# Attention on one core: head-norm roots spread by a TensorE product, value maxima on VectorE, some high parts on GpSimd

## The chip, the cores and the metric

The kernel runs on one core of a Trainium2 chip. The metric is the device time of one execution in microseconds (us); where several runs exist, their median is taken. The core's engines are TensorE (PE, with its weight loads as PEld), VectorE (DVE), ScalarE (ACT), GpSimd (POOL) and SyncE (SP), which here issues nearly all DMA transfers. Each engine works through its own instructions in the order in which they stand in its queue, and waits on semaphores for the others.

## The reference

The input is 1024 positions of 1024 features. Layer 0 is a recurrent block (RG-LRU) and a squared-ReLU MLP; layer 1 is attention in a band of chunks, with keys and values computed from the stream, and a second MLP. The diff touches the attention alone:

```python
def rmsnorm(x, g):
    y = xf * lax.rsqrt(jnp.mean(xf * xf, axis=-1, keepdims=True) + EPS)
    return (y * g).astype(x.dtype)
...
h = rmsnorm(x, kv_norm)
kv = (h @ w_kv).reshape(bsz, s, 2, N_HEADS, HEAD_DIM)      # 16 heads of 64
k = rmsnorm(kv[:, :, 0], k_norm)                           # norm over each head's 64 features
v = kv[:, :, 1]
...
q = rmsnorm((rmsnorm(h, b_norm[j]) @ b_w_q[j]).reshape(bsz, s, N_HEADS, HEAD_DIM), b_q_norm[j])
# 64-row chunks; each sees 9 chunks of keys (8 to the left and its own)
sc = jnp.einsum('bhqd,bhkd->bhqk', qb, kb) * scale + bias
p = jax.nn.softmax(sc, axis=-1)
o = jnp.einsum('bhqk,bhkd->bhqd', p, vb)
h = h + o @ b_w_o[j]
```

Everything is float32, and the result is the whole stream after the second MLP.

## The kernel before, in words

All activations are held transposed: features on the 128 partitions, positions along the row, in halves of 512 (`H2`). Large products are done in three passes of rounded parts, high x high, low x high and high x low (`mm`, L376 to L378); ACT makes a high part by a rounding copy, and VectorE or GpSimd subtracts it to get the low part.

The attention stage works on eight pairs of heads `t`. For each, `Proj` makes keys, queries and values in this order. Each of the six projections (three kinds, two halves of the positions) is 8 fill steps of three matmuls. `normed` takes a projection of keys or queries out of PSUM (L1726), squares it (L1729, L1732; GpSimd subtracts the low part `sl`, L1735) and adds the sums of squares of each head over the partitions with two matmuls against a band of ones (L1744, L1745). The sums of all four projections of a pair land in one PSUM bank (`nm`; there is one such bank, handed round by the semaphore `nms`), head by head in groups of 16 rows. `roots` makes the reciprocal roots of the bank: ACT Ln, Exp and Square, then two VectorE steps (L1794 to L1805). What remains is to spread each head's row of roots over its 64 partitions. For that L1807 writes eight rows to DRAM (`rd`), and four DMA reads (L1811) bring them back, each row repeated 64 times, as four tiles `rb` of 128 x 512. At L1752 VectorE multiplies the projection with its gain and with `rb`. High and low float16 parts follow (L1762, L1768), and eight small transfers that place the two heads of the pair (`moves`).

`values` takes the value projection out of PSUM (L1686) and lets ACT sum its absolute values over the row (L1689); the two sums, added, bound the largest value and give the scale for the float16 parts (`planes`), which DMA transposes turn (L1668).

A `Unit` is one head (`e`), one half of the queries (`h`) and two blocks of 128 queries (`u`); there are 64. `score` computes the scores of one block `qi` in PSUM (L1963, L1964), adds the bias and takes the row's extreme on VectorE (L1967), takes the exponential on ACT (L1974), and, when both blocks' sums have been inverted (`roots` of the unit, L1990 on VectorE and L1992 on GpSimd), makes the high part `hi` on ACT (L1982) and the low part on VectorE (L1984). Two DMA transposes turn the parts (L1668: `t<-t` for the wide units with `h` = 1, `v<-v` for the others), TensorE weighs the values with them (L2010), and `leave` combines the result (L2021, L2023).

The order in which all engines get their instructions is planned at build time. `Plan` holds a clock for every engine, adds an assumed cost for each step (`c_act`, `c_dve`, `c_pool`, `C_MOVE` for a transfer) and an assumed latency, and issues the steps of all chains in the order of these planned times. `TensorE`'s filler is the row of projection steps (and at its end the first steps of the output projection); a unit is begun when the number of filler steps done reaches its due step and one of `ROWS` tickets is free, which it gives back when its scores are done:

```python
total = 8 * 6 * NF + 2 * JP * (NF - 1)
due = [START]
for c in cost:
    due.append(due[-1] + (total - START - LATE) * c / sum(cost))
```

The plan does not see what a transfer or a wait really takes: an instruction that stands early in its engine's queue holds those behind it.

Tiles come from rings: `g` (64 tiles of 128 x 512, among them `q`, `hr`, `rb`), `w` (14 of the same size, for the weights' parts and short-lived results), `raw` (8), and two rings of 128 x 640 for the scores.

Of the kernel before, what the change touches and what calls it, by code (L numbers as in the profile page):

```python
# [9 lines left out]
F32 = mybir.dt.float32  # L10
# [5 lines left out]
P = 128  # L16
T = 1024
D = 1024
NF = 8
# [15 lines left out]
WIDE = {"nm": 1, "s2": 2}  # L35
PIN = 0
WARM = 9
START = 52
LATE = 12
SLACK = 14  # L40
LOAD_O = 24
SPILL = 5
SPARE = 0.1
ROWS = 3
FR = 0.9
LAT = 0.3
LAT0 = 0.1
# [18 lines left out]

def c_act(n):
    return 0.2 + n * 0.00082


def c_acts(n):
    return 0.28 + n * 0.000836


def c_dve(n):
    return 0.145 + n * 0.00105
# [105 lines left out]
def tile_yoco_rglru_chunk_attention(  # L182
# [43 lines left out]
    def gf(s="g"):  # L226
        return gp.tile([P, H2], F32, tag="g", name=nm(s))
# [22 lines left out]
    def rawf():  # L250
        return rp.tile([P, H2], F32, tag="raw", name=nm("raw"))

    def wr(s="w"):
        return wp.tile([P, H2], F32R, tag="w", name=nm(s))

    def wf():
        return wp.tile([P, H2], F32, tag="w", name=nm("wf"))
# [7 lines left out]
    def bank(tag=None):  # L265
        if tag is None:
            tag = ("pj", "tp", "sc", "pj", "tp", "sc", "po", "sc")[ring[0] % 8]
            ring[0] += 1
        if tag in BANKS:
            return ps1.tile([P, H2], F32, tag=tag, name=nm(tag), bufs=BANKS[tag])  # L270
        return loose.tile([P, H2], F32, tag=tag, name=nm(tag), bufs=(LOOSE if tag in LOOSE else WIDE)[tag])
# [1323 lines left out]
    x1d = dp.tile([NF, P, T], F32, name="x1d")  # L1595
    x2d = dp.tile([NF, P, T], F32, name="x2d")
    x3d = dp.tile([NF, P, T], F32, name="x3d")
    rd = dp.tile([NF, 8, H2], F32, name="rd")
    od = dp.tile([SPILL, 2, P, T], F32, name="od")
    hid = dp.tile([7, NQ, P, H2], F32, name="hid")  # L1600

# [60 lines left out]
    def move(dst, src):  # L1662
        dma(dst, src)
        return plan.use("sp", C_ISSUE) + C_MOVE
# [6 lines left out]
    class Proj:  # L1671


        def __init__(self, t):
            self.t = t
            self.Q = self.K = self.KL = None
            self.rb = [None] * 4
            self.split = [0, 0]
            self.added, self.spread = [Flag(plan) for _ in range(4)], [Flag(plan) for _ in range(4)]
            self.VS, self.V = [None, None], [None, None]  # L1680
            self.made = {(kind, h): Flag(plan) for kind in range(3) for h in range(2)}

        def values(self, h, ps):
            yield scaled[h]
            q = gf("q")
            dve.scalar_tensor_tensor(q, ps, -1.0, R[h], ALU.mult, ALU.mult)  # L1686
            yield plan.use("dve", c_dve(H2))
            m = tiny()
            act.activation(rawf(), q, AF.Abs, accum_out=m)  # L1689
            yield plan.use("act", c_act(H2) + 0.19)  # L1690
            self.V[h] = q, m
            if not h:
                return
            t = self.t
            (_, m0), (_, m1) = self.V
            peak, up = tiny(), tiny()
            dve.tensor_scalar(peak, m0, m1, 1e-20, ALU.add, ALU.max)
            dve.reciprocal(up, peak)
            dve.tensor_scalar(up, up, UP, 1.0, ALU.mult, ALU.mult)
            dve.tensor_scalar(vsc[:, t : t + 1], peak, UP ** -2, 1.0, ALU.mult, ALU.mult)  # L1700
            yield plan.use("dve", 0.45)
            for a, b in SIDES:
                act.activation(vsx[a, t : t + 1], vsc[b, t : t + 1], AF.Copy)
                plan.use("act", 0.2)
            for g in range(2):
                plan.start(self.planes(g, self.V[g][0], up))
# [15 lines left out]
        def normed(self, kind, h, ps):  # L1722
            keys = kind == KEYS
            yield scaled[h]
            q = gf("q")
            dve.scalar_tensor_tensor(q, ps, -1.0, R[h], ALU.mult, ALU.mult)  # L1726
            yield plan.use("dve", c_dve(H2))
            sh = wr("sh")
            act.activation(sh, q, AF.Square)  # L1729
            plan.use("act", c_act(H2))  # L1730
            s = wf()
            act.activation(s, q, AF.Square)  # L1732
            yield plan.use("act", c_act(H2))
            sl = wr("sl")
            SLE.tensor_tensor(sl, s, sh.bitcast(F32), ALU.subtract)  # L1735
            yield plan.use("pool", c_pool(2 * H2), True) if SLE is pool else plan.use("dve", c_dve(H2), True)
            j = 2 * kind + h
            if not j:
                yield nms
                self.ss = bank("nm")  # L1740
            else:
                yield self.added[j - 1]
            ones2 = band[:, 96 - 32 * j : 96 - 32 * j + P]
            pe.matmul(self.ss, lhsT=ones2, rhs=sh, start=j == 0, stop=False, skip_group_check=True)  # L1744
            pe.matmul(self.ss, lhsT=ones2, rhs=sl, start=False, stop=j == 3, skip_group_check=True)  # L1745
            yield plan.pe(2 * H2)
            self.added[j].set(plan.t)
            if j == 3:
                plan.start(self.roots())
            yield self.spread[j]  # L1750
            r = self.rb[j]
            dve.scalar_tensor_tensor(q, q, gk if keys else gq, r, ALU.mult, ALU.mult)  # L1752
            yield plan.use("dve", c_dve(H2), True)
            if keys:
                if not h:
                    self.K, self.KL = (gh("ev"), gh("od")), (gh("lo"), gh("los"))
                even, odd, low, lows = (x[:, hs(h)] for x in (*self.K, *self.KL))
            else:
                if not h:
                    self.Q, self.QL = (gh("ev"), gh("od")), gh("lo")  # L1760
                even, odd, low = (x[:, hs(h)] for x in (*self.Q, self.QL))
            act.activation(even, q, AF.Copy)  # L1762
            ready = plan.use("act", c_act(H2))
            if not keys:
                act.activation(odd[OD], q[OD], AF.Copy)
                plan.use("act", c_act(H2))
            yield ready
            dve.tensor_tensor(low, q, even, ALU.subtract)  # L1768
            yield plan.use("dve", c_dve(H2), True)
            self.split[kind] += 1  # L1770
            if self.split[kind] == 2:
                plan.start(self.moves(kind))
# [19 lines left out]
        def roots(self):  # L1792
            ss, r = self.ss, gf("hr")
            act.activation(r, ss, AF.Ln, scale=1.0 / HD, bias=eps)  # L1794
            yield plan.use("act", c_act(H2))
            act.activation(r, r, AF.Exp, scale=-0.5)
            yield plan.use("act", c_act(H2))
            x = wf()
            act.activation(x, r, AF.Square, scale=(0.5 / HD) ** 0.5)
            yield plan.use("act", c_act(H2))  # L1800
            dve.scalar_tensor_tensor(x, ss, HD * EPS, x, ALU.add, ALU.mult)
            last = plan.use("dve", c_dve(H2))
            nms.release(last)
            yield last
            dve.scalar_tensor_tensor(r, x, 1.5, r, ALU.subtract, ALU.mult)  # L1805
            yield plan.use("dve", c_dve(H2), True)
            move(rd[self.t], r[0:P:16])  # L1807
            yield plan.busy["sp"] + C_MOVE
            for j in range(4):
                self.rb[j] = rb = gf("rb")  # L1810
                last = move(  # L1811
                    rb,
                    rd[self.t, 2 * j : 2 * j + 2].unsqueeze(1).broadcast_to([2, HD, H2]),
                )
                self.spread[j].set(last)
            yield last

# [42 lines left out]
    def weight():  # L1860
# [5 lines left out]
            plan.start(prepare())  # L1866
        return w

    def head_gains():
        yield plan.t  # L1870
        dve.tensor_reduce(
            peaks, hn[:, 2:].rearrange("p (g d) -> p g d", g=2), mybir.AxisListType.X, ALU.max,
            apply_absolute_value=True,
        )
        dve.tensor_scalar(peaks, peaks, 1e-15, 1.0, ALU.max, ALU.mult)
        dve.reciprocal(under, peaks)
        dve.tensor_scalar(gq, hn[:, 0:1], under[:, 0:1], UPN, ALU.mult, ALU.mult)
        dve.tensor_scalar(gk, hn[:, 1:2], under[:, 1:2], -UPN, ALU.mult, ALU.mult)
        dve.tensor_scalar(c1, peaks[:, 0:1], peaks[:, 1:2], UPN ** -2 / 8, ALU.mult, ALU.mult)
        dve.reciprocal(nb, c1)  # L1880
        dve.tensor_scalar(nb, nb, -1.0, 1.0, ALU.mult, ALU.mult)
        yield plan.use("dve", 1.4)
# [10 lines left out]
    class Unit:  # L1893
# [54 lines left out]
        def score(self, qi):  # L1948
# [30 lines left out]
                self.pieces = self.plane(), self.plane()  # L1979
            off = qi * self.count[0] * P  # L1980
            hi, lo = (x[:, off : off + wdt] for x in self.pieces)
            act.activation(hi, sc[:, :wdt], AF.Copy, scale=sm)  # L1982
            yield plan.use("act", c_acts(wdt))
            dve.scalar_tensor_tensor(lo, sc[:, :wdt], sm, hi, ALU.mult, ALU.subtract)  # L1984
            self.scored[qi].set(plan.use("dve", c_dve(wdt) + 0.06, True))

# [395 lines left out]
```

## Time and profile before

| | |
|---|---|
| two runs | 2226.83 and 2232.08 us, median 2229.45 |
| the profiled execution | 2225.27 us, span 2223.2 |
| TensorE busy, matmul | 2027.9 us, 91% of the span |
| VectorE busy | 1490.2 us, 67% |
| ScalarE busy | 1104.1 us, 50% |
| GpSimd busy | 436.3 us, 20% |
| mean granted clock of TensorE | 0.958 |

A row of a list of groups reads: line, engine, operation, output<-input by the program's names, shapes, count, busy time in us, mean ns of one, idle time of the engine before them and what ended it. A row of the order of time reads: start in us, duration, engine, line, operation, and in brackets how long the engine sat idle before it and what released it. A row of the chain that ended last reads: start, duration, what. A row of a table of stretches gives, for each engine, busy us and the number of instructions, then granted clock, DMA share and GB/s. `x11` is a count. For one line's instructions, three durations in ns are least, median and greatest.

### The profile page before, as it was taken

How to read it: one execution, taken by the hardware profiler on the slowest of the kernel's cores; microseconds unless marked ns; L12 is line 12 of the kernel's file. 1: busy time of each engine (PE TensorE's matmuls, PEld its weight loads, DVE VectorE, ACT ScalarE, POOL GpSimd, SP SyncE). 2: the span in 40 equal slices, each digit the busy share in tenths (PEclk: the TensorE clock that was granted, in tenths of full speed). 3: DMA queues.
4: the chain of work that ended last, by engine and by line, in shares of the span. 5: the costliest groups of instructions: out<-in, count | busy, mean ns of one | idle time of the engine just before them, and what ended most of it. 6: DMA issues, size and time to landing. Idle time of an engine off the chain costs nothing.

```text
span 2223.2 us, 27860 instructions
## 1 busy us (share of the span) xinstructions
PE 2027.9 (91%) x9209; PEld 1638.1 (74%) x9209; DVE 1490.2 (67%) x2340; ACT 1104.1 (50%) x1920; POOL 436.3 (20%) x429
## 2 busy tenths in 40 slices
PE   7999999999999999977687769539999999999999
PEld 6888888888888888855465546427888888888887
DVE  6898777666777766345655456357886667777743
ACT  6778454434345455435575457356553434444532
POOL 2000113222200001332443334311123223000000
PEclk9999999999999999988898889869999999999999
DMA  4012435444697835247777656868444444887833
GB/s 156 29 44 83 147 117 182 156 148 146 220 333 241 262 127 176 86 75 121 128 154 142 133 117 154 192 126 188 158 159 152 157 156 157 317 279 243 252 106 104
DMA packets 319297, 357.07 MB, mean 161 GB/s; under 512 B 163952, under 2 KB 166896, under 8 KB 319152
## 3 DMA queue, kind: packets, MB, share of 16 engines
q1 hardware_dynamic: 319008, 355.24, 56.0%
q8 instruction: 72, 1.18, 0.2%
q14 instruction: 73, 0.60, 0.1%
q10 hardware_dynamic: 144, 0.05, 0.0%
HBM read 230.28 MB, written 80.87 MB: 140 GB/s over the span
## 4 chain that ended last, share of the span: by engine, by line
PE 79%; DMA 11%; DVE 3%; SPq 2%; issue 2%; ACT 2%; POOL 2%; DVEq 0%; POOLq 0%; ACTq 0%
PE pj L376 11%; PE pj L377 11%; PE pj L378 11%; PE tp L377 5%; PE tp L378 5%; PE tp L376 5%; DMA rb<-rd 5%; PE p L377 4%; PE sc L376 4%; PE sc L377 4%; PE p L378 4%; PE sc L378 4%; PE p L376 4%; PE po L2010 2%; DMA t<-t 1%
## 5 line engine op out<-in xcount | busy, mean ns | idle before, releaser
L376 PE MATMUL pj<-h,wh 128*128 128x512 f32 x1260 | 511.8, 406 | 7.3 <-ACT h L2032 7.2
L377 PE MATMUL pj<-l,wh 128*128 128x512 f32 x1260 | 497.6, 395 | 0.8 <-DVE l L2034 0.8
L378 PE MATMUL pj<-h,wl 128*128 128x512 f32 x1260 | 497.4, 395 | 0.0
L1140 ACT ACTIVATE wh<-raw 128x512 fp32r<-128x512 f32 x333 | 205.6, 624 | 168.7 <-PE pj L377 43.5
L376 PEld LDWEIGHTS pj<-h,wh 128*128 128x128 f32 x1260 | 242.0, 192 | 59.5 <-ACT h L2032 8.0
L1141 DVE TENSOR_TENSOR wl<-raw,wh 128x512 fp32r<-128x512 f32 x333 | 254.0, 770 | 39.3 <-ACT wh L1140 36.2
L378 PEld LDWEIGHTS pj<-h,wl 128*128 128x128 f32 x1260 | 240.7, 191 | 52.0
L377 PEld LDWEIGHTS pj<-l,wh 128*128 128x128 f32 x1260 | 241.7, 192 | 49.4 <-DVE l L2034 1.5
L389 ACT ACTIVATE h<-raw 128x512 fp32r<-128x512 f32 x224 | 139.3, 628 | 217.5 <-PE sc L377 61.8
L378 PE MATMUL tp<-h,wl 128*128 128x512 f32 x554 | 215.7, 389 | 1.5 <-DVE wl L342 1.5
L377 PE MATMUL tp<-l,wh 128*128 128x512 f32 x554 | 215.8, 389 | 0.3 <-DVE l L390 0.3
L376 PE MATMUL tp<-h,wh 128*128 128x512 f32 x554 | 215.6, 389 | 0.0
L390 DVE TENSOR_TENSOR l<-raw,h 128x512 fp32r<-128x512 f32 x224 | 153.5, 692 | 76.1 <-ACT h L389 73.1
L1415 ACT ACTIVATE s<-s 128x512 f32<-128x512 f32 x125 | 79.0, 633 | 203.7 <-DVE s L1414 195.0
L2010 PEld LDWEIGHTS <-vs 128*128 128x128 f16 x576 | 53.5, 103 | 157.4 <-issue 131.0
L377 PE MATMUL p<-l,wh 128*128 128x512 f32 x384 | 150.7, 392 | 9.3 <-DVE l L672 9.3
L376 PE MATMUL sc<-h,wh 128*128 128x512 f32 x394 | 153.3, 389 | 0.0
L378 PE MATMUL sc<-h,wl 128*128 128x512 f32 x394 | 153.3, 389 | 0.0
L377 PE MATMUL sc<-l,wh 128*128 128x512 f32 x394 | 153.3, 389 | 0.0
L376 PE MATMUL p<-h,wh 128*128 128x512 f32 x384 | 151.1, 393 | 1.0 <-ACT wh L555 1.0
L378 PE MATMUL p<-h,wl 128*128 128x512 f32 x384 | 150.3, 391 | 0.0
L1149 POOL TENSOR_TENSOR raw<-raw,raw 128x512 f32<-128x512 f32 x29 | 49.9, 1721 | 372.1 <-DVE wl L1141 274.0
(323 smaller groups left out, 3599.2 us busy)
## 6 DMA issues: line engine op xcount, KB each, us to landing
raw<-hid SPq DMA_DIRECT2D x224, 256.0 KB
hid<-s SPq DMA_DIRECT2D x221, 256.0 KB
raw<-in_w_down SPq DMA_DIRECT2D x192, 256.0 KB
raw<-in_w_up SPq DMA_DIRECT2D x128, 256.0 KB
s<-in_w_down SPq DMA_DIRECT2D x64, 256.0 KB
raw<-in_w_kv SPq DMA_DIRECT2D x32, 256.0 KB
rb<-rd SPq DMA_DIRECT2D x32, 256.0 KB
raw<-in_w_in SPq DMA_DIRECT2D x30, 256.0 KB
```

Source lines behind the costliest of these rows:

```text
L376: pe.matmul(ps, lhsT=wh, rhs=xh, start=start, stop=False, skip_group_check=more)
L377: pe.matmul(ps, lhsT=wh, rhs=xl, start=False, stop=False, skip_group_check=more)
L378: pe.matmul(ps, lhsT=wl, rhs=xh, start=False, stop=stop, skip_group_check=more)
L389: act.activation(h, src, AF.Copy)
L390: dve.tensor_tensor(l, src, h.bitcast(F32), ALU.subtract)
L1140: act.activation(wh, raw, AF.Copy)
L1141: dve.tensor_tensor(wl, raw, wh.bitcast(F32), ALU.subtract)
L1149: pool.tensor_tensor(raw[A11], raw[A11], raw[A21], ALU.add)
L1415: act.activation(out, out, AF.Square)
L2010: pe.matmul(dst, lhsT=st, rhs=src, start=start, stop=final, skip_group_check=self.u == 1)
```

## The change

The roots no longer go through DRAM. After the last VectorE step of `roots`, ACT rounds the whole tile to a high part `rh`, and one VectorE step forms `rr`: the high part in a group's first eight rows and the remainder, with `lows` = -1, in row 8 of each group of 16. For each of the four projections TensorE then multiplies `rr` with a constant matrix `pick[:, j]`, which has ones where a head's high row and its remainder row meet the head's 64 partitions; the product lands in the `nm` bank, and L1752's VectorE step reads it from there and gives the bank back. `pick` (a tile of the `w` ring, held for the whole stage) and `lows` are built at the start of the stage in `head_gains`.

The largest absolute value comes from a VectorE reduction instead of an ACT sum, and the larger of the two halves' results is taken instead of their sum. The high part of the second block (`qi` = 1) of the units with `h` = 1, 32 steps of 128 x 640, moves from ACT to GpSimd. The first unit is due after 48 filler steps instead of 52, and four units instead of three may be in their score phase.

```diff
-START = 52
+START = 48
-ROWS = 3
+ROWS = 4
+def c_phi(n):
+    return 0.08 + n * 0.001
...
             m = tiny()
-            act.activation(rawf(), q, AF.Abs, accum_out=m)
-            yield plan.use("act", c_act(H2) + 0.19)
+            dve.tensor_reduce(m, q, mybir.AxisListType.X, ALU.max, apply_absolute_value=True)
+            yield plan.use("dve", c_dve(H2))
...
-            dve.tensor_scalar(peak, m0, m1, 1e-20, ALU.add, ALU.max)
+            dve.tensor_scalar(peak, m0, m1, 1e-20, ALU.max, ALU.max)
...
             yield self.spread[j]
-            r = self.rb[j]
+            yield nms
+            r = bank("nm")
+            pe.matmul(r, lhsT=pick[:, j, :], rhs=self.rr, start=True, stop=True)
+            yield plan.pe(H2)
             dve.scalar_tensor_tensor(q, q, gk if keys else gq, r, ALU.mult, ALU.mult)
-            yield plan.use("dve", c_dve(H2), True)
+            last = plan.use("dve", c_dve(H2))
+            nms.release(last)
+            yield last
...
             dve.scalar_tensor_tensor(r, x, 1.5, r, ALU.subtract, ALU.mult)
             yield plan.use("dve", c_dve(H2), True)
-            move(rd[self.t], r[0:P:16])
-            yield plan.busy["sp"] + C_MOVE
+            hi, self.rr = wr("rh"), wr("rr")
+            act.activation(hi, r, AF.Copy)
+            yield plan.use("act", c_act(H2))
+            dve.scalar_tensor_tensor(self.rr, hi.bitcast(F32), lows, r, ALU.mult, ALU.add)
+            last = plan.use("dve", c_dve(H2), True)
             for j in range(4):
-                self.rb[j] = rb = gf("rb")
-                last = move(
-                    rb,
-                    rd[self.t, 2 * j : 2 * j + 2].unsqueeze(1).broadcast_to([2, HD, H2]),
-                )
                 self.spread[j].set(last)
...
+    pick, lows = wr("pick").rearrange("p (j m) -> p j m", j=4), kp.tile([P, 1], F32, name="lows")
     def head_gains():
         yield plan.t
+        where = wf().rearrange("p (j m) -> p j m", j=4)
+        pool.memset(where, 0.0)
+        for low in range(2):
+            for e, half in enumerate((EV, OD)):
+                pool.affine_select(
+                    out=where[:, :, half], in_=where[:, :, half], pattern=[[-32, 4], [0, HD]],
+                    compare_op=ALU.not_equal, fill=1.0, base=-16 * e - 8 * low, channel_multiplier=1,
+                )
+        act.activation(pick, where, AF.Copy)
+        mark = gf("mark")
+        pool.memset(mark[:, :HD], 0.0)
+        pool.affine_select(... fill=-1.0, base=-8, channel_multiplier=1)
+        plan.use("pool", 5.0)
+        dve.tensor_reduce(lows, mark[:, :HD], mybir.AxisListType.X, ALU.add)
...
-            act.activation(hi, sc[:, :wdt], AF.Copy, scale=sm)
-            yield plan.use("act", c_acts(wdt))
+            if h and qi:
+                pool.tensor_scalar(hi, sc[:, :wdt], sm, 1.0, ALU.mult, ALU.mult)
+                yield plan.use("pool", c_phi(wdt), True)
+            else:
+                act.activation(hi, sc[:, :wdt], AF.Copy, scale=sm)
+                yield plan.use("act", c_acts(wdt))
```

More of the change, by code (lines that the diff above doesn't have):

```diff
@@ L1597, in tile_yoco_rglru_chunk_attention @@
     x3d = dp.tile([NF, P, T], F32, name="x3d")
-    rd = dp.tile([NF, 8, H2], F32, name="rd")
     od = dp.tile([SPILL, 2, P, T], F32, name="od")
@@ L1676, in __init__ @@
             self.Q = self.K = self.KL = None
-            self.rb = [None] * 4
             self.split = [0, 0]
@@ L1867, in weight @@
         return w
+    pick, lows = wr("pick").rearrange("p (j m) -> p j m", j=4), kp.tile([P, 1], F32, name="lows")
     def head_gains():
         yield plan.t
+        where = wf().rearrange("p (j m) -> p j m", j=4)
[9 more added lines that the diff above has]
+        pool.memset(mark[:, :HD], 0.0)
+        pool.affine_select(
+            out=mark[:, :HD], in_=mark[:, :HD], pattern=[[-16, 8], [-1, 8]],
+            compare_op=ALU.not_equal, fill=-1.0, base=-8, channel_multiplier=1,
+        )
+        plan.use("pool", 5.0)
+        dve.tensor_reduce(lows, mark[:, :HD], mybir.AxisListType.X, ALU.add)
         dve.tensor_reduce(
```

## The prediction

> **What bounds the kernel now.** I read the page first: the busy tenths, the DMA line under them and the shares of the chain that ended last.
>
> ```profile
> span 2223.2 us, 27860 instructions
> PE   7999999999999999977687769539999999999999
> DMA  4012435444697835247777656868444444887833
> PE pj L376 11%; PE pj L377 11%; PE pj L378 11%; PE tp L377 5%; PE tp L378 5%; PE tp L376 5%; DMA rb<-rd 5%; PE p L377 4%; PE sc L376 4%; PE sc L377 4%; PE p L378 4%; PE sc L378 4%; PE p L376 4%; PE po L2010 2%; DMA t<-t 1%
> ```
>
> TensorE is full everywhere but in slices 18 to 28, about 945 to 1556 us: the attention stage, the only one the diff touches. There the DMA engines are busier than in the slices around it. The chain is TensorE nearly throughout; its largest other item is the transfer `rb<-rd`, the spreading of the head-norm roots that this change removes. Next, the waits of TensorE between 900 and 1600 us and one wait of VectorE (columns: sum in us, times, longest).
>
> ```profile
> PE po L2010 <- DMA t<-t: 76.4, 14, 20.5
> PE po L2010 <- DMA v<-v: 40.3, 9, 18.7
> PE nm L1745 <- POOL sl L1735: 28.6, 6, 16.3
> PE s L1963 <- DVE t L1967: 6.6, 6, 2.4
> DVE q L1752 <- DMA rb<-rd: 119.5, 32, 4.8
> ```
>
> TensorE is said to wait for transposes, not for the roots. The order of time says what lies behind it. These are the waits of TensorE that are longer than 10 us, one for each of the eight head pairs:
>
> ```profile
> 978.69 0.80 PE L1745 MATMUL nm<-sl,band 128*128 128x512 f32 x1 [16.32 <-POOL sl L1735]
> 1040.95 0.80 PE L2010 MATMUL po<-v,vs 128*128 128x256 f16 x4 [12.00 <-DVE o L2023]
> 1108.97 0.37 PE L2010 MATMUL po<-t,vs 128*128 128x256 f16 x1 [16.04 <-DMA t<-t]
> 1179.18 0.37 PE L2010 MATMUL po<-t,vs 128*128 128x256 f16 x1 [14.26 <-DMA t<-t]
> 1260.32 0.37 PE L2010 MATMUL po<-v,vs 128*128 128x256 f16 x1 [15.23 <-DMA v<-v]
> 1324.29 0.40 PE L2010 MATMUL po<-t,vs 128*128 128x256 f16 x1 [16.64 <-DMA t<-t]
> 1408.43 0.37 PE L2010 MATMUL po<-v,vs 128*128 128x256 f16 x1 [18.72 <-DMA v<-v]
> 1483.54 0.37 PE L2010 MATMUL po<-t,vs 128*128 128x256 f16 x1 [20.49 <-DMA t<-t]
> ```
>
> They add up to 129.7 us. I looked into the third, from 1093 to 1109: SyncE's queue, VectorE, and the busy times of that stretch (PE, PEld, DVE, ACT, POOL, then granted clock, DMA share, GB/s).
>
> ```profile
> 1084.02 9.23 SPq L286 DMA_DIRECT2D rb<-rd  x4
> 1093.36 14.69 SPq L1668 DMA_TRANSPOSE t<-t  x2
> 1091.76 0.75 DVE L1752 SCALAR_TENSOR_TENSOR q<-q,gk,rb 128x512 f32<-128x512 f32 x1 [1.34 <-DMA rb<-rd]
> 1107.80 0.75 DVE L1752 SCALAR_TENSOR_TENSOR q<-q,gq,rb 128x512 f32<-128x512 f32 x1 [3.80 <-DMA rb<-rd]
> 1093.00:1109.00 16.00, 0.03 (x1) 0.03 (x1) 4.34 (x8) 1.38 (x3) 1.26 (x1) 0.60 0.88 76
> ```
>
> Four products `q*rb` stand between 1091.76 and 1107.80, so 5.35 us apart: that is the pace at which the four reads of 256 KB land, one behind the other. VectorE works in order and is held by each; SyncE is held for 9.23 us by the four issues and for 14.69 us by the two transposes behind them; TensorE wants those transposes. All five engines stand still, and for one reason.
>
> **What goes.** One `rd` write and four `rb` reads for each pair, 40 transfers, leave SyncE's queue, and four buffers of the g ring are no longer taken. A transpose that has no `rb` reads ahead of it is quick:
>
> ```profile
> 1016.92 3.51 DMA t<-t
> L1668 SPq DMA_TRANSPOSE t<-t x64: 1259/1484/10807, 1005.3 to 1541.6; - x64
> ```
>
> It lands 3.51 us after its start, and half the issues take at most 1.484 us. In the third stall, issued where the reads now are (1084.02), two transposes would land near 1084.0 + 2 x 1.5 + 3.5 = 1090.5, before TensorE arrived at 1092.9. So nothing else was close behind, and I count all eight stalls as gone: **-129.7**. What is late next are the lags of ACT, POOL and DVE, priced below. As the stall holds every engine, none of them used it to catch up with TensorE much, which is why I don't give the time back to them.
>
> After each such stall TensorE is slow for a while. The first two rows are eleven products after a stall and after none, the other two the start of the first and fourth projection product after a stall; behind them, the pace of a full stage.
>
> ```profile
> 1110.10 2.08 PE L2010 MATMUL po<-t,vs 128*128 128x256 f16 x11 [0.75 <-DMA t<-t]
> 1020.47 1.15 PE po L2010 x11
> 1111.93 0.78 PE L376 MATMUL pj<-h,wh 128*128 128x512 f32 x1
> 1113.36 0.42 PE L376 MATMUL pj<-h,wh 128*128 128x512 f32 x1
> 100.00:200.00 100.00, 100.00 (x443) 82.81 (x442) 95.41 (x99) 72.97 (x81) 3.98 (x4) 1.00 0.16 51
> ```
>
> The products cost 2.08 - 1.15 = 0.93 more; three projections take 1.43 instead of 3 x 100/443 = 0.68, 0.75 more. Together 1.68, eight times: **-13.4**.
>
> **What comes on TensorE.** 32 products of 512 columns, of a kind and size with the projections: 32 x 100/443 = **+7.2**, and nothing hides them, TensorE being the chain. Each also adds a wait. The product for j = 0 needs the roots, now with two more steps (the ACT copy `rh` and the VectorE step `rr`); those for j = 1 to 3 need the one `nm` bank back, so the VectorE product before them. Behind such a product on TensorE stand projections, scores and weighings; behind the VectorE step that waits for it stand the subtractions `lo` and all reductions. How late the roots come shows in the last sum of a pair and the end of its roots, in the first pair and in the last:
>
> ```profile
> 943.34 0.40 PE L1745 MATMUL nm<-sl,band 128*128 128x512 f32 x1
> 947.97 0.69 DVE L1805 SCALAR_TENSOR_TENSOR hr<-wf,hr 128x512 f32<-128x512 f32 x1
> 1433.47 0.40 PE L1745 MATMUL nm<-sl,band 128*128 128x512 f32 x1
> 1453.10 0.67 DVE L1805 SCALAR_TENSOR_TENSOR hr<-wf,hr 128x512 f32<-128x512 f32 x1
> ```
>
> With idle engines the roots take 5.3 us (943.34 to 948.66), in the last pair 20.3 (1433.47 to 1453.77). The planner sets the product where it thinks the roots done; only the lag behind its plan is waited out. Where TensorE today depends directly on another engine, the rows of waits give that lag: the five shorter waits for `sl` are (28.6 - 16.3)/5 = 2.5 us, the longest wait of a score for VectorE 2.4. Bounds: nothing, and 20.3 - 5.3 = 15 us for a pair. I take 2.5 for j = 0, the nearest row, and 0.5 for each of the other three, whose VectorE step is issued right behind: 4 us for a pair, **+32**.
>
> **Work that moves between ACT, DVE and POOL.**
>
> ```profile
> L1982 ACT ACTIVATE t<-sc,t 128x640 f16<-128x640 f32 x64 | 49.0, 817 | 11.7 <-POOL t L1992 11.7
> L1888 POOL TENSOR_SCALAR s<-s,heads 128x640 f32<-128x640 f32 x16 | 16.8, 1048 | 148.3 <-DMA s<-in_relb 115.7 <-PE po L2010 30.8 <-issue 0.9
> L1689 ACT ACTIVATE raw<-q 128x512 f32<-128x512 f32 x16 | 10.0, 624 | 5.6 <-DVE q L1686 5.6
> L1686 DVE SCALAR_TENSOR_TENSOR q<-pj,rneg 128x512 f32<-128x512 f32 x16 | 11.0, 688 | 16.6 <-PE pj L378 16.4
> ```
>
> For each pair ACT loses four wide high parts (4 x 0.817) and two absolute sums (2 x 0.624), and gains `rh` (0.62): 3.9 us less. POOL gains four high parts; no row shows one, a scaling of the same shape costs it 1.048, so 4.2 us. VectorE gains two maxima and `rr` at about 0.69: 2.1 us. A maximum is bounded by a 512-wide VectorE step on one side and nothing on the other. The row of the fourth pair shows the room:
>
> ```profile
> 1110.00:1180.00 70.00, 50.74 (x263) 37.84 (x263) 37.12 (x76) 42.40 (x87) 26.39 (x30) 0.87 0.76 141
> ```
>
> From the third long wait to the eighth, five pairs take 374.6 us, 74.9 each; by the terms above that becomes 74.9 - 16.2 - 1.7 + 0.9 + 4 = 62. VectorE would then be busy 39 of 62 us, ACT 38.5, POOL 30.6, TensorE near 51: no engine but TensorE becomes the bound. **0** here; cover is that the others have a quarter or more idle, and if it fails it shows as longer lags, the 15 us bound above. The high parts on POOL are 0.2 us slower in a chain of about six steps that the planner spreads out.
>
> A rule speaks against that move. VectorE's low parts at L1984 read two operands in SBUF:
>
> ```profile
> L1984 DVE SCALAR_TENSOR_TENSOR t<-sc,t,t x64: 859/879/1975, 1004.6 to 1537.4; 128x640 f16<-128x640 f32 x64
> ```
>
> Half take at most 0.879, one 1.975: something holds one for 1.1 us. The Trainium skill, "SBUF — State Buffer", section "Who interferes with whom", says that a VectorE instruction with two SBUF inputs and a GpSimd instruction that reads SBUF exclude each other for the whole instruction, the later one waiting. The spread of that row agrees with it.
>
> New constants at build time: the marks take POOL two memsets and five selections for which no row stands. POOL idled 12.35 us at that point, so they are hidden if they stay below that:
>
> ```profile
> 919.23 0.91 POOL L1888 TENSOR_SCALAR s<-s,heads 128x640 f32<-128x640 f32 x1 [12.35 <-DMA s<-in_relb]
> ```
>
> A permanently held w buffer, units begun four steps earlier (START) and a fourth unit in its score phase (ROWS) change the order alone. At most they take or give a pair's lag of 2.5 us, +-20 in all; I put them at 0.
>
> **Sum**, against the profiled execution's 2225.3 (span 2223.2 and 2.1 around it): 2225.3 - 129.7 - 13.4 + 7.2 + 32 = 2121.4. That execution is 4 below the median of the two runs shown, which are 5 apart; I forecast **2120**.
>
> **Rivals.**
> *TensorE waits for the roots.* The wait in place of the one removed: the lag is not 2.5 but most of the loaded chain, say 9 us for j = 0 and 1 for each other, 12 for a pair. Then 2121.4 + 64 = 2185 at the far end, 2150 to 2185 in all. For it: the 20.3 us. Against: the planner counts load too.
> *The lock on VectorE and POOL decides.* 32 more POOL steps each hold a VectorE step for up to 1.1 us, 36 us, all on the path: 2157. Against: VectorE has a quarter idle.
> *The transposes are the limit by themselves.* The stalls stay under the same names, as SyncE still issues every one of them; only half of the 143 is won: 2193. If none is, 2225 + 7 = 2232. Against: the 3.51 us.
> *Slower than before.* One `nm` bank makes the four products a relay between TensorE and a crowded VectorE. The gain is 143 - 7 = 136 us over 32 products: from 4.2 us of wait for each, the kernel is slower, and at 6 us, 2225 - 136 + 192 = 2281. Against: 2.4 us is the longest today.
> *Better than forecast.* No new waits: 2089; with the 20 of the order, 2070.
>
> **Chances.** Forecast (2090 to 2150) 0.6; better 0.1; roots 0.12; lock 0.06; transposes 0.08; slower 0.04. The range of 2072 to 2168 holds the forecast, better but for its edge, lock and half of roots, so a little over 0.8. A measurement of this kernel can tell about 2% from no change: below 2185 is faster. Forecast, better, lock, roots and a little of the transposes: 0.88 faster, 0.08 within 2%, 0.04 slower.
>
> **What will show it.** Right: no row `rb<-rd`; no TensorE wait above 10 us between 945 and 1450; no `DMA_TRANSPOSE` issue near 10 us; a pair's period near 62 us; granted clock above 0.9 in the stage; new waits of TensorE for `rr` and L1752, 2 to 3 us for a pair's first. Wrong: waits of 8 us or more for `rr` (roots), the median of L1984 well over 0.879 with TensorE waiting behind it (lock), or waits for `t<-t` and `v<-v` still over 40 us in sum (transposes).

## The result, and the profile after

The changed kernel took 2071.16 us (median of 2069.05 and 2073.28) against 2229.45 before. Timed again in rounds it took 2071.34 against 2224.54: a ratio of 0.931, with a 95% interval of 0.930 to 0.933. The profiled execution took 2073.28 us. The forecast was 2120, with a range from 2072 to 2168: right in direction, but it saw 109 us of a gain of 158, and the time came out just below the range.

The page of the changed kernel, the same parts as before the change (span, TensorE by slice, DMA by slice, the chain):

```profile
span 2071.5 us, 27888 instructions
PE   9999999999999999999999899689999999999999
DMA  5112426434489783533677777785444436987732
PE pj L380 11%; PE pj L382 11%; PE pj L381 11%; PE tp L381 6%; PE tp L382 6%; PE tp L380 6%; PE p L380 4%; PE p L381 4%; PE p L382 4%; PE sc L380 4%; PE sc L381 4%; PE sc L382 4%; DMA raw<-in_w_down 1%; DVE t L2012 1%; DVE sc L1991 1%
```

Two things changed in the TensorE row. The holes of slices 18 to 28 are nearly closed; a remnant stands near slice 26. And the first slice went from 7 to 9, at a place that no line of the diff seems to touch. `rb<-rd` has left the chain. Now the waits of TensorE in the attention stage (sum in us, times, longest), the six largest, of which the last is one that the prediction asked for. Then the stretch of time in which all engines stood still before; the changed kernel is at a later point of its work there (PE, PEld, DVE, ACT, POOL, granted clock, DMA share, GB/s):

```profile
PE po L2038 <- DMA t<-t: 12.6, 12, 2.4
PE s L1987 <- DVE t L1991: 10.5, 6, 6.2
PE s L1987 <- DMA ev<-lo: 6.4, 2, 5.3
PE po L2038 <- DVE o L2051: 3.1, 4, 1.6
PE nm L1747 <- POOL sl L1737: 2.7, 4, 1.2
PE nm L1755 <- DVE q L1757: 2.6, 3, 1.5
```

```profile
1093.00:1109.00 16.00, 15.78 (x92) 11.46 (x91) 15.78 (x32) 9.14 (x21) 7.01 (x7) 1.00 0.94 169
```

No wait is above 10 us. All waits of the stage add up to 41.6 us instead of 177.6, of which the eight long ones were 129.7 and the others 47.9. The new products wait 2.6 us for the bank, the sums of squares another 1.3 for the same bank while VectorE reads a product from it; no row of TensorE's waits names `rr`. The DMA share reads 0.94 in that stretch while TensorE is busy for 15.78 of its 16 us, so a high share is no sign of the bound by itself. Of the other signs that the prediction named, a pair takes 54.1 us (first product of the third pair to that of the eighth, a fifth of 1313.59 - 1043.16) where 62 were forecast, the longest issue of a transpose is 3.95 us instead of 10.8, and the granted clock of the stage is 0.96 instead of 0.86.

### The profile page after: what moved, and what is told of

The parts are those of the page before. It is cut to its first block, busy times and chain, and to the rows that moved or that the text cites. A ratio compares the mean times of both kernels' runs of the same rounds, so it can differ in the third digit from the quotient of the medians.

```text
span 2071.5 us, 27888 instructions
## 1 busy us (share of the span) xinstructions
PE 2020.6 (98%) x9241; PEld 1632.1 (79%) x9241; DVE 1516.2 (73%) x2365; ACT 1076.4 (52%) x1865; POOL 485.5 (23%) x468
## 4 chain that ended last, share of the span: by engine, by line
PE 82%; DVE 7%; DMA 5%; issue 2%; POOL 2%; ACT 2%; SPq 1%; DVEq 0%; POOLq 0%; ACTq 0%
PE pj L380 11%; PE pj L382 11%; PE pj L381 11%; PE tp L381 6%; PE tp L382 6%; PE tp L380 6%; PE p L380 4%; PE p L381 4%; PE p L382 4%; PE sc L380 4%; PE sc L381 4%; PE sc L382 4%; DMA raw<-in_w_down 1%; DVE t L2012 1%; DVE sc L1991 1%
## 5 line engine op out<-in xcount | busy, mean ns | idle before, releaser
L380 PE MATMUL pj<-h,wh 128*128 128x512 f32 x1260 | 503.6, 400 | 0.0
L381 PE MATMUL pj<-l,wh 128*128 128x512 f32 x1260 | 492.3, 391 | 0.0
L340 POOL TENSOR_TENSOR raw<-raw,vec 128x512 f32<-128x512 f32 x48 | 63.1, 1315 | 281.2 <-DMA raw<-in_w_kv 280.9
```

The lines of the kernel that those rows point to most:

```text
L340: pool.tensor_tensor(raw, raw, gains, ALU.mult)
L380: pe.matmul(ps, lhsT=wh, rhs=xh, start=start, stop=False, skip_group_check=more)
L381: pe.matmul(ps, lhsT=wh, rhs=xl, start=False, stop=False, skip_group_check=more)
```

## The experiments

A ratio is to the kernel before, timed in the same comparison. The line numbers are each kernel's own.

**Roots alone, and all but the roots.** The first is the changed kernel with these edits taken back:

```diff
-START = 48
+START = 52
-ROWS = 4
+ROWS = 3
...
-            dve.tensor_reduce(m, q, ..., ALU.max, apply_absolute_value=True)
+            act.activation(rawf(), q, AF.Abs, accum_out=m)
...
-            dve.tensor_scalar(peak, m0, m1, 1e-20, ALU.max, ALU.max)
+            dve.tensor_scalar(peak, m0, m1, 1e-20, ALU.add, ALU.max)
...
-            if h and qi:
+            if False:
```

The second has these edits and the roots of before.

> The kernel before with one part of the change: the roots spread by TensorE (START 52, ROWS 3, absolute sums and all high parts on ACT as before). Theory A: the eight long stalls go, the new products cost TensorE next to no waiting, and the other edits are worth little: 2075 to 2095 us. Theory B: the terms of the prediction were right for this part (2121) and the other edits, put at 0 there, brought the other 50: 2105 to 2135 us.

> The kernel before with every part but the roots, which still go through DRAM. Theory A: the eight waits of TensorE above 10 us stay, 2205 to 2235 us. Theory B: 2170 to 2190 us.

Roots alone: 2082.98 us, ratio 0.934 (0.933 to 0.936). All but the roots: 2228.54, ratio 1.000 (0.999 to 1.001). Theory A holds in its main part: all but the roots keeps eight waits of TensorE above 10 us (10.4 to 20.4), and roots alone has none. That the other edits are worth little is so where the roots go through DRAM; what they are worth beside the product stands below. The waits of TensorE in the stage of roots alone are 48.8 us, and its rows for the new product are these:

```profile
PE nm L1755 <- DVE q L1757: 0.3, 2, 0.2
PE nm L1755 <- DVE rr L1817: 0.3, 1, 0.3
```

So the part that the prediction priced at +32 costs 0.6 us of waiting. Roots alone also holds a side effect of the new constants, shown under "The first slice", that has nothing to do with the roots.

**Why the reads were slow.** Each root stands in 16 rows of the tile anyhow. This kernel writes all of them and lets a read take 32 rows four times instead of 2 rows 64 times; it reads the same bytes into the same tile, and writes 256 KB instead of 16.

```diff
-    rd = dp.tile([NF, 8, H2], F32, name="rd")
+    rd = dp.tile([NF, P, H2], F32, name="rd")
...
-            move(rd[self.t], r[0:P:16])
+            move(rd[self.t], r)
...
-                    rd[self.t, 2 * j : 2 * j + 2].unsqueeze(1).broadcast_to([2, HD, H2]),
+                    rd[self.t, 32 * j : 32 * j + 32].unsqueeze(1).broadcast_to([32, 4, H2]),
```

> The kernel before; all 128 rows of roots are written to DRAM instead of 8 (each root stands in 16 of them anyhow), and each read takes 32 rows four times instead of 2 rows 64 times. Same bytes read, 256 KB a read. Theory C: the reads were slow (5.35 us each, 49 GB/s) because of their pattern with 2 rows outermost; now the four products at L1752 follow each other within 3 us, the stalls mostly go, 2095 to 2145 us. Rival D: the trip through DRAM and SyncE's queue is what costs; the pace of the reads stays near 5 us or the waits above 10 us stay, 2210 to 2235 us.

> All parts of the change but the roots, with the 32-row reads of the other kernel. Theory C: 2070 to 2115 us, near the changed kernel without any product of TensorE. Rival D: as all but the roots, above 2170 us.

2095.35 us, ratio 0.940 (0.939 to 0.942); with the other edits 2094.84, ratio 0.940 (0.939 to 0.941). Theory C holds, though the products took 3.6 us where 3 were expected. In the first of the two, SyncE's issue of the four reads of a pair, the VectorE products that use them, and the last line of the answer on the tile `rb`:

```profile
1108.75 2.71 SPq L286 DMA_DIRECT2D rb<-rd  x4
1114.55 0.75 DVE L1752 SCALAR_TENSOR_TENSOR q<-q,gk,rb 128x512 f32<-128x512 f32 x1
1116.09 0.73 DVE L1752 SCALAR_TENSOR_TENSOR q<-q,gk,rb 128x512 f32<-128x512 f32 x1
1116.74 1.41 DVE L1752 SCALAR_TENSOR_TENSOR q<-q,gq,rb 128x512 f32<-128x512 f32 x2
DMA to landing us min/median/max: 3.0/3.7/5.3
```

The four products are over in 3.6 us instead of 16.8, and none waits for `rb`. SyncE is free after 2.7 us instead of 9.2. The Trainium skill, "DMA: Bandwidth & Descriptors", section "Rules for kernel authors", says that an outermost dimension of c < 16, such as two rows each broadcast, confines a transfer to at most c of the 16 DMA engines. The traces agree. These are stretches in which almost nothing but such reads moves, in the kernel before and in the one with 32 rows (PE, PEld, DVE, ACT, POOL, granted clock, DMA share, GB/s):

```profile
1099.00:1107.00 8.00, 0.00 (x0) 0.00 (x0) 1.55 (x3) 0.00 (x0) 0.00 (x0) 0.50 0.13 49
1111.00:1113.00 2.00, 2.00 (x18) 1.52 (x18) 2.00 (x3) 0.29 (x2) 1.98 (x2) 1.00 0.89 277
```

With 2 rows outermost 0.13 of 16 engines is the work of two; with 32 rows it is that of 14, and at 277 GB/s a read takes about 1 us (an estimate, 262 KB / 277) instead of 5.35. The packets themselves were no slower with 2 rows: 193 of them took 13.0% of 16 engines over those 8 us, about 86 ns each, and 306 took 88.8% over those 2 us, about 93 ns each. So reading the same two rows again and again was not what cost. The 0.88 of DMA share in the prediction's stretch from 1093 to 1109 hid this: it comes from the microsecond from 1098 to 1099, where the share reads 10.35, which no share of busy time can be.

**The first slice.** In the kernel before, the head-gain steps of VectorE stood at place 9 of its queue, among the splits of the input, and waited for a transfer of 65 KB. These are VectorE and TensorE of the kernel before, in order of time:

```profile
18.71 0.28 DVE L1871 TENSOR_REDUCE heads<-hn 128x2 f32<-128x128 f32 x1 [9.35 <-DMA hn<-in_hnorm]
20.36 0.79 PE L377 MATMUL p<-l,wh 128*128 128x512 f32 x1 [9.31 <-DVE l L672]
```

In the changed kernel the new constants stand ahead of these steps, and they stay at place 953:

```profile
L1895 DVE TENSOR_REDUCE heads<-hn x1: 277/277/277, 910.2 to 910.2; 128x2 f32<-128x128 f32 x1
```

Two kernels exchange just that. The first is the kernel before with a dummy of `lows` ahead, the second the changed kernel with the constants behind the gains:

```diff
+    lows = kp.tile([P, 1], F32, name="lows")
+
     def head_gains():
         yield plan.t
+        mark = gf("mark")
+        pool.memset(mark[:, :HD], 0.0)
+        dve.tensor_reduce(lows, mark[:, :HD], mybir.AxisListType.X, ALU.add)
```

> The kernel before with nothing of the change but one side effect: a small tile marked by GpSimd and reduced by VectorE stands ahead of the head-gain steps, as in the changed kernel, so that these stay at the start of the attention stage in VectorE's queue (place 953) and don't stand at place 9 of it, where they wait for the gains' transfer. Theory E: VectorE is held 9.35 us there at the start of the execution, TensorE 9.3 us, and nothing takes it back later: 2217 to 2222 us against 2229. Rival: the early loads are late anyhow, within 3 us of before.

> The changed kernel with the new constants behind the head-gain steps, so that these go back to place 9 of VectorE's queue. Theory E: 2079 to 2083 us, TensorE waiting 9 us near 20 us. Rival: 2071 as the changed kernel.

2213.7 us, ratio 0.994 (0.992 to 0.995), and 2083.04, ratio 0.936 (0.934 to 0.937), which is 12 above the changed kernel. TensorE's waits in the first 45 us are 11.3 us before, 1.5 in the first of the two, 10.3 in the second and 1.6 in the changed kernel. Theory E is shown: 10 to 12 us of the gain are a side effect of where the new constants were written. The first of the two gained 12 us, a little more than theory E's 7 to 12 below 2229. Roots alone has this side effect too; the two kernels with 32-row reads above do not.

**The other edits.** The high parts on GpSimd and the order constants are taken back from the changed kernel, each by itself; the maximum on VectorE was not tried by itself. The edits of the first two kernels:

```diff
-            if h and qi:
+            if False:
```

```diff
-START = 48
+START = 52
-ROWS = 4
+ROWS = 3
```

> The changed kernel with all high parts on ACT. Theory A (the other edits bring the 12 us between roots alone and the whole change): with this one taken back 2073 to 2080 us. If the lock between VectorE and GpSimd cost something, it is faster than 2071; if ACT's relief is the whole of the 12 us, 2083.

> The changed kernel with START 52 and ROWS 3. Theory A: 2073 to 2083 us, the order brings some of the 12 us that the other edits add to roots alone; prediction's value, nothing: 2071.

> The changed kernel with ROWS 3, START 48. Tells which of the two constants brought the 14 us: 2083 to 2087 if it is ROWS, 2069 to 2074 if it is START.

> The changed kernel with START 44: a search for a faster one. If the first units profit from being due earlier still, 2060 to 2068; if they wait for keys that are not made, 2071 to 2085.

> The changed kernel itself, timed against before in rounds, as the point from which the other runs are counted: 2069 to 2075 us if its two first runs stand for it; if 2078 or more, the differences of 4 to 18 us that were laid to the other edits shrink by as much.

> The changed kernel with START 52 and ROWS 4, the fourth corner beside START 48 with ROWS 4 (2071), 48 with 3 (2089) and 52 with 3 (2085). If the fourth ticket is what brings the order's gain, 2069 to 2077; if the two constants only work together, 2082 to 2090.

> Roots alone, beside the changed kernel in one comparison: 2081 to 2086 us, 10 to 14 more than the changed kernel, if the other edits together bring that; the same as the changed kernel if they bring nothing.

| kernel | us | ratio, 95% interval |
|---|---|---|
| changed kernel again | 2071.34 | 0.931 (0.930 to 0.933) |
| roots alone, in the same comparison | 2081.45 | 0.936 (0.934 to 0.938) |
| high parts on ACT | 2075.15 | 0.932 (0.931 to 0.934) |
| START 52, ROWS 4, with the first two rows | 2075.14 | 0.933 (0.931 to 0.935) |
| START 52, ROWS 3 | 2085.26 | 0.937 (0.936 to 0.938) |
| START 48, ROWS 3 | 2088.97 | 0.938 (0.936 to 0.940) |
| START 44, ROWS 4 | 2080.79 | 0.935 (0.933 to 0.937) |

The rows come from three comparisons, and the kernel before took between 2224.5 and 2226.8 us in them, so differences of 4 us or less between rows of different comparisons say nothing. The fourth ticket is worth 9 to 18 us (times and ratios) with START 52 or 48; START 48 against 52, and GpSimd's high parts, are not told from nothing. START 44 is 8 to 9 us slower than 48, for a reason that was not sought. The two kernels with ROWS 3 came 2 us above the ranges expected. With ROWS 3 and START 52 all waits of TensorE in the stage are 55.6 us instead of 41.6, nearly the whole difference.

The other edits together bring 10 us where TensorE spreads the roots, and nothing where the roots go through DRAM: not in all but the roots (2228.54), and not with the 32-row reads, where the long stalls are gone too (2094.84 against 2095.35). So it is not the end of the stalls alone that lets them pay; what in the DRAM trip keeps them from it stays open. None of these kernels is faster than the changed one.

**What the head of TensorE's queue costs.** The work is the same, but the planner believes `rh` and `rr` free, so the products stand earlier in the queue:

```diff
             act.activation(hi, r, AF.Copy)
-            yield plan.use("act", c_act(H2))
+            plan.use("act", c_act(H2))
             dve.scalar_tensor_tensor(self.rr, hi.bitcast(F32), lows, r, ALU.mult, ALU.add)
-            last = plan.use("dve", c_dve(H2), True)
+            plan.use("dve", c_dve(H2), True)
+            last = plan.t
```

> The changed kernel, but the planner is told that the two last steps of the roots (rh on ACT, rr on VectorE) take no time, so that the spreading products stand earlier in TensorE's queue; the work is the same. Theory F (the waits priced at +32 did not come because the plan counts the queues in front of ACT and VectorE and sets the products behind the real end of the roots, 2 us or so late): set early, TensorE waits for rr, 2 to 5 us for a pair, 2085 to 2110 us. Rival G (TensorE has slack there, whatever the place): 2069 to 2076 us.

2096.1 us, ratio 0.942 (0.940 to 0.943), 23 to 25 above the changed kernel. Its waits of TensorE for the product:

```profile
PE nm L1755 <- DVE rr L1817: 18.5, 8, 4.9
PE nm L1755 <- DVE q L1757: 3.1, 1, 3.1
```

Theory F holds: the mechanism that the prediction feared exists, 2.3 us a time, when the product is placed early. In all eight pairs TensorE then starts the first product 0.05 to 0.06 us after the end of `rr`.

**A well-shaped DRAM trip against the product,** everything else as changed: the 32-row reads, the other edits and the late gains.

> All parts of the change but the roots, these through DRAM with 32 rows outermost, and the head-gain steps late. What is left between this and the changed kernel is the TensorE product against a well-shaped DRAM trip: theory C and E together give 2095 - 12 = 2083 us; if the product's shorter way is worth nothing, 2071.

2083.94 us, ratio 0.936 (0.935 to 0.938). With the other edits in place the product is worth 11 to 13 us over a good trip through DRAM. Without them it is worth nothing that shows: the 32-row reads took 2095.35 us, and less the 12 us of the late gains that is 2083 (an estimate; that kernel was not run), where roots alone took 2081.45 and 2082.98. The largest waits of TensorE in this kernel are for transfers, which the changed kernel has less of:

```profile
PE po L2023 <- DMA v<-v: 13.9, 8, 5.6
PE s L1972 <- DMA ev<-lo: 13.8, 3, 9.2
```

## Why the prediction was wrong, point by point

**The eight stalls, -129.7: right.** None is left, and roots alone took them away. The account of their cause was right as far as it went, a slow read that holds VectorE, SyncE and the transposes; why it was slow was not asked.

**The slow clock after a stall, -13.4: right in size.** TensorE's busy time fell from 2027.9 to 2020.6 us although 7.2 were added, so the same products took 14.5 us less, by an estimate that takes the forecast 7.2 as given; it was not measured apart.

**The new waits, +32: the step that failed.** It measured 3.9 us in the changed kernel (2.6 and 1.3, all for the bank) and 0.6 in roots alone. The prediction took the lag at which TensorE met other engines today, 2.5 us, for the time by which the product would stand ahead of the end of its input. In the changed kernel, last sum, end of the roots and first product of the fifth pair:

```profile
1127.57 0.40 PE L1747 MATMUL nm<-sl,band 128*128 128x512 f32 x1
1144.55 0.74 DVE L1817 SCALAR_TENSOR_TENSOR rr<-rh,lows,hr 128x512 fp32r<-128x512 f32 x1
1145.91 0.39 PE L1755 MATMUL nm<-rr,pick 128*128 128x512 f32 x1
```

The roots take 17.7 us from sum to `rr` (15.4 before in this pair, without the two new steps), so a loaded chain is as slow as feared, but the product stands 0.6 us behind its end. In all eight pairs it stands 0.05 to 1.7 us behind, and no wait of a product for `rr` is counted. That the plan manages this by counting the queues is argued from its code; shown is that the waits come when the same product is placed earlier.

**Order constants, 0 within 20: inside the bound, on the wrong value.** Taken back together, the two constants cost 14 us, and it is the fourth ticket that brings it.

**Not in the sum at all: the start of the execution.** The prediction called TensorE full everywhere but in slices 18 to 28 and looked only at the stage that the diff names; TensorE's waits in the first 45 us fell by 9.7. The first digit 7 of the busy tenths stood in its own first fence.

Together, for the profiled executions: 129.7 + 6.3 (other waits of the stage, 47.9 to 41.6) + 9.7 + 7.3 (busy time) = 153.0, less 0.8 by which small waits elsewhere grew, against the 152.0 us that went. The forecast had 103.9. What it lacked is 28.1 of new waits that did not come (32 to 3.9), 10.2 by which the old short waits fell (47.9 to 37.7), the 9.7 and 1.1 of clock. The order constants are within these waits, as their 14 us above show.

**The costs of moved work: right.** The new constants took GpSimd 2.5 us. The maximum took 0.675 us (0.69 taken), the high part on GpSimd 1.034 (1.048 taken):

```profile
L1691 DVE TENSOR_REDUCE t<-q 128x1 f32<-128x512 f32 x16 | 10.8, 675 | 0.1
L2007 POOL TENSOR_SCALAR t<-sc,t 128x640 f16<-128x640 f32 x32 | 33.1, 1034 | 2.2
L2012 DVE SCALAR_TENSOR_TENSOR t<-sc,t,t 128x640 f16<-128x640 f32 x64 | 76.6, 1216 | 11.0 <-POOL t L2007 6.4 <-ACT t L2010 4.3
```

**The rivals.** Roots: the wait was there only when the product was placed early. Lock: the low parts rose from 66.0 us in all before to 76.6, and with the high parts back on ACT they took 67.0, so the move costs VectorE about 10 us; but the kernel was not faster then (2075.15), so this cost did not decide. Transposes: TensorE's waits for `t<-t` and `v<-v` fell from 116.7 to 13.4 us, and with only the reads reshaped to 20.7; they were victims. Slower: not so. "Better than forecast", given 0.1, is what came. That its 2070 is so near is partly luck: it has no term for the start of the execution, and the order gave 14 us, not 20.

## What to carry to other kernels

When a transfer holds several engines at once, ask why the transfer itself is slow before replacing it: changing the shape of its access pattern gave 133 of the 153 to 158 us here, without a new instruction. Another 10 to 12 are the start of the execution, and the new product pays for itself only together with the fourth ticket and the other edits. A wait at the head of an in-order queue is priced by where the planner sets the instruction against the real end of its input, not by how long that input takes. And read the whole row of busy tenths, for an edit can move instructions at the other end of the kernel.

## What the runs showed of the hardware that was not expected

DRAM reads of 256 KB with 2 rows outermost and repeated followed each other every 5.35 us, at 49 GB/s and with a DMA share of 0.13, the work of two engines of 16; with 32 rows outermost such reads moved 277 GB/s at a share of 0.89, and one landed 3.7 us (median) after its issue. While the slow reads ran, transposes behind them in SyncE's queue took up to 10.8 us to issue. A DMA share over a long stretch can mislead: 0.88 from 1093 to 1109 was 0.13 in the half of it from 1099 to 1107.
